# A hybrid decoder layer on one core: where TensorE's operands start, and how the FFN columns are cut

## The chip, the core and the metric

The kernel runs on one core of a Trainium2 chip, as one program in one launch. The metric is the time on the device in microseconds, and the lower one is better. Three runs before the change took 1976.21, 1979.71 and 1979.8 us; the median is 1979.71.

## The reference

One layer on x of 256 tokens by 2048 columns, in float32:

```python
h = x
h = h + 0.5 * swiglu(rms_norm(h, ffn1_norm), w_gate1, w_up1, w_down1)
p = rms_norm(h, mix_norm) @ w_in
h = h + concat([rwkv7_time_mix(p[:, :3360]), rglru_mix(p[:, 3360:])]) @ w_out
h = h + 0.5 * swiglu(rms_norm(h, ffn2_norm), w_gate2, w_up2, w_down2)
out = rms_norm(h, final_norm)
# swiglu(x, g, u, d) = (silu(x @ g) * (x @ u)) @ d
```

The FFNs are 5632 columns wide (11 x 512). The mixer between them has two recurrences over the tokens. Its own code is not touched by the change.

## The kernel before, in words

Every large product is made in three parts. An operand is split into a float32r tile `hi` and the rest `lo`, and hi x hi, hi x lo and lo x hi are added in PSUM. The weights come from DRAM through `weights` (L47): SP issues a DMA of 1 MB into a tile `wst`, of which there are three; ACT casts it to `whi` (L73), DVE subtracts and writes `wlo` (L74), each at most 1024 columns, three tiles of each. `rows_times` (L85) then makes one k (128 rows of the weights): for both row tiles of 128 tokens and each cut of up to 512 columns, the activations are the stationary operand (128 x 128) and the weights the moving one.

`ffn` (L164) cuts the 5632 columns into chunks of 1024, 1024, 1024, 1024, 768 and 768. For each chunk it makes gate over 16 k, then silu on ACT, then up over 16 k, then their product `hid` on DVE. `hidden_T` (L178) turns `hid` with TensorE transposes inside the next chunk's gate (the last chunk's inside the down projection) and splits it into hThi and hTlo. A 768 wide chunk has a cut of 512 and one of 256. After the chunks comes the down projection over 44 k.

The first FFN's stationary operand is `xa` (xahi, xalo), made by `transposed_half` (L126): TensorE transposes x, four blocks for each pair of a k and a PSUM bank half, ACT scales and rounds into xahi (L143), DVE writes the rest into xalo (L144). x comes in four DMAs of 512 columns. The second FFN's stationary operand is `xb`. In the mixer's projections, `columns_times` (L97), the roles are swapped: the weights are stationary, and 256 tokens of xa move.

A scheduler sets the order on each engine, by priorities that the code gives (`high_priority`: the larger offset goes first) and by `issue_after`, which keeps an instruction behind another on its queue.

Where a tile starts follows from the sizes of the tiles before it. In the built program the constants (identity and ones of 512 bytes per partition, gains of 192, `junk` of 2048, small ones) end 22,400 bytes into a partition, and the weights' pool starts there: 1920 bytes past a multiple of 2048. The weights' tiles, xa, h, hT and `hid` all have sizes that keep this remainder, so all of them start 1920 past. The tiles of the right side are packed from the other end: there xb and the second h start 2016 past. Within xa and xb a stationary slice starts at a further multiple of 512, within the weights' tiles a moving one at a multiple of 2048 (with the 768 wide chunks too, one k to a tile).

Of the kernel before, what the change touches and what calls it, by code (L numbers as in the profile page):

```python
# [3 lines left out]

# [7 lines left out]
F32 = mybir.dt.float32  # L12
# [8 lines left out]
class Core:  # L21


    def __init__(self, ctx, tc, S, D, WMAX):
        self.tc, self.nc = tc, tc.nc
        self.S, self.D = S, D
        self.NT, self.NK = S // P, D // P
        self.WMAX = WMAX
        self.const = ctx.enter_context(tc.tile_pool(name="const", bufs=1))
        self.wpool = ctx.enter_context(tc.tile_pool(name="wpool", bufs=3))  # L30
        self.psum = ctx.enter_context(tc.tile_pool(name="psum", bufs=1, space=PSUM))
        self.uid = 0
# [3 lines left out]
        self.h = None  # L36
        self.ones = self.const.tile([P, P], F32, name="ones")
        nc.gpsimd.memset(self.ones, 1.0)
# [7 lines left out]

    def weights(self, pieces, ktiles, kstep=2, kop=1, head=False):  # L47


        nc = self.nc  # L50
        width = sum(w for _, _, w in pieces)
        steps = [1, 1] if head else []
        while sum(steps) < len(ktiles):
            steps.append(min(kstep, len(ktiles) - sum(steps)))
        for k0, n in zip(itertools.accumulate([0] + steps), steps):
            with self.tc.high_priority(offset=4000):
                st = self.wpool.tile([P, 2 * self.WMAX], F32, name=self.name("wst"), tag="wst")
                stv = st[:, : n * width].rearrange("p (k f) -> p k f", k=n)
                kk = ktiles[k0]
                at = 0  # L60
                for mat, c0, w in pieces:
                    nc.sync.dma_start(
                        out=stv[:, :, at : at + w],
                        in_=mat[kk * P : (kk + n) * P, c0 : c0 + w].rearrange("(k p) f -> p k f", p=P),
                    )
                    at += w
                parts = []
                for j in range(0, n, kop):
                    m = min(kop, n - j)
# [3 lines left out]
                    self.last_split = nc.scalar.copy(hi[:, : m * width], src)  # L73
                    nc.vector.tensor_tensor(  # L74
                        lo[:, : m * width], src, hi[:, : m * width].bitcast(F32), ALU.subtract
                    )
                    parts.append((hi, lo))
# [7 lines left out]
    def rows_times(self, banks, xhi, xlo, kidx, whi, wlo, width, first, last):  # L85

        nc = self.nc
        for t in range(self.NT):
# [5 lines left out]
            for n, c, w in cuts:  # L94
                nc.tensor.matmul(banks[t][n][:, :w], b, whi[:, c : c + w], start=False, stop=last)  # L95

# [28 lines left out]

    def transposed_half(self, hf, gT, xhi, xlo, banks):  # L126

        nc = self.nc
        per = self.NK // 2
        for j in range(0, per, 2):  # L130
            bk = self.bank(banks[(j // 2) % len(banks)])
            for jj in range(2):
                k = hf * per + j + jj
                for t in range(self.NT):
                    nc.tensor.transpose(  # L135
                        bk[:, jj * 256 + t * P : jj * 256 + (t + 1) * P],
                        self.h[:, t, k * P : (k + 1) * P],
                        self.ident,
                    )
            for jj in range(2):  # L140
                k = hf * per + j + jj
                src = bk[:, jj * 256 : jj * 256 + self.S]
                nc.scalar.activation(xhi[:, k, :], src, AF.Copy, scale=gT[:, k : k + 1])  # L143
                nc.vector.scalar_tensor_tensor(  # L144
                    xlo[:, k, :], src, gT[:, k : k + 1], xhi[:, k, :].bitcast(F32), ALU.mult, ALU.subtract
                )

    def sumsq(self, c0, w, acc, junk):
# [14 lines left out]

def ffn(core, xhi, xlo, rstd, wg, wu, wd, after_first, after_down, fpool, down, head=False):  # L164
    nc, NT, NK, D, S = core.nc, core.NT, core.NK, core.D, core.S
# [3 lines left out]
    while c < DFF:  # L169
        left = DFF - c  # L170
        w = 1024 if left >= 2 * 1024 or left <= 1024 else left // 2
        w = min(w, left)
        chunks.append((c, w))
        c += w
# [22 lines left out]
    for c0, w in chunks:  # L197
        nb = (w + 511) // 512
        cuts = [(n, n * 512, min(512, w - n * 512)) for n in range(nb)]
        gb = [[core.bank(t * nb + n) for n in range(nb)] for t in range(NT)]  # L200
        for i, (k, hi, lo) in enumerate(core.weights([(wg, c0, w)], ks, head=head and c0 == 0)):
            core.rows_times(gb, xhi, xlo, k, hi, lo, w, i == 0, i == NK - 1)
            if i == NK // 2 - 1:
                for f in pending:
# [20 lines left out]
    for piece, (c0, w) in enumerate(down):  # L225
        nb = w // 512
        db = [[core.bank((bank0 + t * nb + n) % 8) for n in range(nb)] for t in range(NT)]
        bank0 += NT * nb
        for i, (k, hi, lo) in enumerate(core.weights([(wd, c0, w)], list(range(NF)), 2048 // w, 1024 // w)):
            core.rows_times(db, hT_hi, hT_lo, k, hi, lo, w, i == 0, i == NF - 1)  # L230
# [17 lines left out]
class Mix:  # L248
# [170 lines left out]
    def project(self, pieces, ntile, xhi, xlo):  # L419
# [6 lines left out]
        for i, (k, hi, lo) in enumerate(core.weights(pieces, list(range(NK)), 4, 2)):  # L426
            core.columns_times(bks, ntile, i, i == NK - 1, xhi, xlo, k, hi, lo)
# [481 lines left out]
def kernel(ctx: ExitStack, tc: tile.TileContext, dram: dict, out: bass.AP):  # L909
# [23 lines left out]
    def norm_half(i, hf, xhi, xlo):  # L933
        core.transposed_half(hf, gT[:, i * NK : (i + 1) * NK], xhi, xlo, (0, 1, 2, 3) if hf == 0 else (4, 5, 6, 7))

# [11 lines left out]
    with ExitStack() as front:  # L947
        xa = xt_pool(front, "xa")
        with ExitStack() as st:
# [19 lines left out]
            def park(hf):  # L969
# [5 lines left out]
            ffn(core, *xa, rstd[0], dram["ffn1_w_gate"][0], dram["ffn1_w_up"][0], dram["ffn1_w_down"][0],  # L975
                first_norm, park, fpool, [(0, HD), (HD, HD)], head=True)
# [66 lines left out]
```

## Time and profile before

| what | us |
|---|---|
| median of the runs | 1979.71 |
| profiled execution | 1979.79 |
| its span, first to last instruction | 1978.1 |
| PE busy (matmuls) | 1952.5 |
| DVE busy | 1078.4 |
| ACT busy | 880.1 |
| head, to the first product | 12.7 |
| first FFN, gate and up | 496.3 |
| second FFN, gate and up | 504.0 |

The stages follow each other on TensorE: gate and up of the first FFN from 12.7 to 509.0, its down projection to 751.7, the mixer to 1122.8, the output projection to 1221.7, gate and up of the second FFN to 1725.7, its down projection to 1966.2. Matmuls are pipelined, so the duration of one overlaps the next; what a matmul costs is read from the start of one to the start of the next, or from a whole stretch over its count.

### The profile page before, as it was taken

How to read it: one execution, taken by the hardware profiler on the slowest of the kernel's cores; microseconds unless marked ns; L12 is line 12 of the kernel's file. 1: busy time of each engine (PE TensorE's matmuls, PEld its weight loads, DVE VectorE, ACT ScalarE, POOL GpSimd, SP SyncE). 2: the span in 40 equal slices, each digit the busy share in tenths (PEclk: the TensorE clock that was granted, in tenths of full speed). 3: DMA queues.
4: the chain of work that ended last, by engine and by line, in shares of the span. 5: the costliest groups of instructions: out<-in, count | busy, mean ns of one | idle time of the engine just before them, and what ended most of it. 6: DMA issues, size and time to landing. Idle time of an engine off the chain costs nothing.

```text
span 1978.1 us, 26035 instructions
## 1 busy us (share of the span) xinstructions
PE 1952.5 (99%) x10789; PEld 1652.5 (84%) x10789; DVE 1078.4 (55%) x1313; ACT 880.1 (44%) x1062; POOL 8.9 (0%) x52
## 2 busy tenths in 40 slices
PE   8999999999999999999999999999999999999997
PEld 6888888888888889898899878888888888888886
DVE  4455444544545447886684875444545455544543
ACT  4544434444434335544354554434443444443443
POOL 0000000000000001000000000000000000000000
PEclk9999999999999999999999999999999999999999
DMA  6555555566656556544342365555555556665553
GB/s 234 192 189 194 182 196 181 167 189 180 209 187 211 191 187 219 164 139 126 97 147 88 127 224 183 189 192 174 188 187 175 181 175 178 207 214 193 193 192 128
DMA packets 128639, 354.51 MB, mean 179 GB/s; under 512 B 21023, under 2 KB 23272, under 8 KB 128392
## 3 DMA queue, kind: packets, MB, share of 16 engines
q1 hardware_dynamic: 128200, 351.79, 55.4%
q8 instruction: 84, 1.38, 0.3%
q10 hardware_dynamic: 320, 1.06, 0.1%
q14 instruction: 35, 0.29, 0.0%
HBM read 347.05 MB, written 5.77 MB: 178 GB/s over the span
## 4 chain that ended last, share of the span: by engine, by line
PE 97%; DVE 1%; ACT 1%; DMA 0%; issue 0%; SPq 0%; DVEq 0%; ACTq 0%
PE bank L92 26%; PE bank L95 26%; PE bank L93 26%; PE bank L104 4%; PE bank L106 4%; PE bank L105 4%; PE bank L183 1%; PE bank L574 1%; PE bank L502 1%; PE bank L467 0%; PE bank L663 0%; PE bank L135 0%; PE bank L691 0%; PE bank L670 0%; DMA wst<-in_ffn_w_gate_dram 0%
## 5 line engine op out<-in xcount | busy, mean ns | idle before, releaser
L74 DVE TENSOR_TENSOR wlo<-wst,whi 128x1024 fp32r<-128x1024 f32 (+1 forms) x680 | 795.5, 1170 | 834.1 <-ACT whi L73 832.9
L73 ACT CAST whi<-wst 128x1024 fp32r<-128x1024 f32 (+1 forms) x680 | 685.8, 1009 | 1004.5 <-PE bank L95 867.3
L92 PE MATMUL bank<-whi,xahi 128*128 128x512 f32 (+1 forms) x896 | 337.2, 377 | 3.8 <-DVE xalo L144 3.6
L93 PE MATMUL bank<-wlo,xahi 128*128 128x512 f32 (+1 forms) x896 | 330.1, 375 | 1.1 <-DVE wlo L74 1.1
L92 PE MATMUL bank<-whi,xbhi 128*128 128x512 f32 (+1 forms) x768 | 289.5, 377 | 0.0
L93 PE MATMUL bank<-wlo,xbhi 128*128 128x512 f32 (+1 forms) x768 | 283.7, 377 | 0.0
L92 PE MATMUL bank<-whi,hThi 128*128 128x512 f32 x704 | 274.2, 390 | 0.0
L93 PE MATMUL bank<-wlo,hThi 128*128 128x512 f32 x704 | 274.0, 389 | 0.0
L95 PE MATMUL bank<-whi,xalo 128*128 128x512 f32 (+1 forms) x896 | 264.8, 376 | 0.0
L95 PE MATMUL bank<-whi,hTlo 128*128 128x512 f32 x704 | 231.4, 389 | 0.0
L95 PE MATMUL bank<-whi,xblo 128*128 128x512 f32 (+1 forms) x768 | 227.6, 377 | 0.0
L92 PEld LDWEIGHTS bank<-whi,xahi 128*128 128x128 f32 x896 | 168.7, 188 | 41.2 <-DVE xalo L144 4.0
L104 PE MATMUL bank<-xahi,whi 128*128 128x256 f32 x688 | 198.6, 289 | 1.0 <-DVE raw L437 1.0
L106 PE MATMUL bank<-xahi,wlo 128*128 128x256 f32 x688 | 197.4, 288 | 0.0
L105 PE MATMUL bank<-xalo,whi 128*128 128x256 f32 x688 | 196.8, 286 | 0.0
L93 PEld LDWEIGHTS bank<-wlo,xahi 128*128 128x128 f32 x896 | 168.6, 188 | 31.9 <-DVE wlo L74 1.5
L95 PEld LDWEIGHTS bank<-whi,xalo 128*128 128x128 f32 x896 | 159.8, 189 | 24.9
L92 PEld LDWEIGHTS bank<-whi,xbhi 128*128 128x128 f32 x768 | 144.5, 188 | 34.3
L93 PEld LDWEIGHTS bank<-wlo,xbhi 128*128 128x128 f32 x768 | 144.4, 188 | 28.7
L95 PEld LDWEIGHTS bank<-whi,xblo 128*128 128x128 f32 x768 | 135.8, 189 | 23.4
L92 PEld LDWEIGHTS bank<-whi,hThi 128*128 128x128 f32 x704 | 132.2, 188 | 27.4
L93 PEld LDWEIGHTS bank<-wlo,hThi 128*128 128x128 f32 x704 | 132.2, 188 | 27.3
(242 smaller groups left out, 1355.3 us busy)
## 6 DMA issues: line engine op xcount, KB each, us to landing
wst<-in_ffn_w_down_dram SPq DMA_DIRECT2D x88, 1024.0 KB, 5.0
wst<-in_ffn_w_up_dram SPq DMA_DIRECT2D x64, 1024.0 KB, 5.0
wst<-in_ffn_w_gate_dram SPq DMA_DIRECT2D x63, 1024.0 KB, 5.0
wst<-in_w_in_dram SPq DMA_DIRECT2D x40, 1024.0 KB, 5.2
wst<-in_ffn_w_gate_dram SPq DMA_DIRECT2D x32, 768.0 KB, 4.4
wst<-in_ffn_w_up_dram SPq DMA_DIRECT2D x32, 768.0 KB, 4.4
wst<-in_w_out_dram SPq DMA_DIRECT2D x16, 1024.0 KB, 5.5
wst<-in_w_in_dram SPq DMA_DIRECT2D x4, 640.0 KB, 4.3
```

The lines of the kernel that those rows point to most:

```text
L73: self.last_split = nc.scalar.copy(hi[:, : m * width], src)
L74: nc.vector.tensor_tensor(lo[:, : m * width], src, hi[:, : m * width].bitcast(F32), ALU.subtract)
L92: nc.tensor.matmul(banks[t][n][:, :w], a, whi[:, c : c + w], start=first, stop=False)
L93: nc.tensor.matmul(banks[t][n][:, :w], a, wlo[:, c : c + w], start=False, stop=False)
L95: nc.tensor.matmul(banks[t][n][:, :w], b, whi[:, c : c + w], start=False, stop=last)
L104: nc.tensor.matmul(out, a, xhi[:, k, :], start=first, stop=False, skip_group_check=True)
L105: nc.tensor.matmul(out, a, xlo[:, k, :], start=False, stop=False, skip_group_check=True)
L106: nc.tensor.matmul(out, b, xhi[:, k, :], start=False, stop=last, skip_group_check=True)
L183: nc.tensor.transpose(bk[:, jj * 256 + t * P : jj * 256 + (t + 1) * P], hid[:, t, (j + jj) * P : (j + jj + 1) * P], core.ident,)
L502: self.nc.tensor.matmul(bk[0:8, :256], ind[:, j0 + j, :], src[:, j * 256 : (j + 1) * 256], start=j == 0, stop=j == 3)
L574: nc.tensor.matmul(bks[par][:, j * P : (j + 1) * P], BK[j // 2][rows, j % 2, c, :], KR[j // 2][rows, j % 2, c, :], start=True, stop=True,)
```

## The change

Three edits are made together.

- Placement: `junk` is 64 bfloat16 elements longer (128 bytes), so that the weights' pool and what follows it start at multiples of 2048 bytes; the second h gets 504 more elements (2016 bytes), so that xb does too. The constants (the identity), and the mixer's own tiles aren't moved to such multiples.
- Chunks: the 5632 columns are cut into 512 and five of 1024. A 512 wide chunk puts two k into one `whi`/`wlo` tile and four k into one DMA; `weights` works this out from the width. Elsewhere its steps stay as they were.
- Head: the first two k of the first gate come as DMAs of one k each, then one of two k; they are asked for alternately with x's quarters, weights first. x is transposed by quarters (`transposed`): the first before the first product, each later one behind the products of k0, k1 and k2 in turn. The splits of k1 to k7 are kept behind the xahi and xalo of given quarters (`marks`).

```diff
-    def weights(self, pieces, ktiles, kstep=2, kop=1, head=False):
+    def weights(self, pieces, ktiles, head=False):
         width = sum(w for _, _, w in pieces)
-        steps = [1, 1] if head else []
+        kop = self.WMAX // width
+        kstep = 2 * kop
+        steps = [1, 1, 2] if head else []
...
-            with self.tc.high_priority(offset=4000):
+            with self.tc.high_priority(offset={0: 9500, 1: 8700, 2: 8500}.get(k0, 4000) if head else 4000):
...
+                    with ExitStack() as behind:
+                        if head and 0 < k0 < 8:
+                            for mark in self.marks[4 * k0 - 1 if k0 < 3 else -1]:
+                                behind.enter_context(self.tc.issue_after(mark.ins))
...
-        left = DFF - c
-        w = 1024 if left >= 2 * 1024 or left <= 1024 else left // 2
-        w = min(w, left)
+        w = (DFF - c) % 1024 or 1024
...
+            if head and c0 == 0 and i in head:
+                with core.tc.high_priority(offset=3000), core.tc.issue_after(core.last_mm.ins):
+                    head[i]()
...
-    junk = const.tile([P, HD], mybir.dt.bfloat16, name="junk")
+    junk = const.tile([P, HD + 64], mybir.dt.bfloat16, name="junk")
...
-                with tc.high_priority(offset=8000 if q < 2 else 0):
+                with tc.high_priority(offset=(9000, 8600, 8400, 8300)[q]):
...
-            with tc.high_priority(offset=8500):
-                norm_half(0, 0, *xa)
-            norm_half(0, 1, *xa)
+            def norm_quarter(q):
+                core.transposed(4 * q, 4, gT[:, :NK], *xa, ((2, 3), (4, 5), (6, 7))[q % 3])
+
+            with tc.high_priority(offset=8800):
+                norm_quarter(0)
...
-        core.h = h2.tile([P, core.NT, D], F32, name="h2")
+        core.h = h2.tile([P, core.NT * D + 504], F32, name="h2")[:, : core.NT * D].rearrange("p (t d) -> p t d", t=core.NT)
```

On SP, the queue of the DMAs, the program begins before with two quarters of x (`h<-in_x`), then weights (`wst`; the sizes are partitions x k x columns):

```order
L958 DMA h_109<-in_x_dram 128x2x512 x2
L62 DMA wst_197<-in_ffn_w_gate_dram 128x1024
L62 DMA wst_215<-in_ffn_w_gate_dram 128x1024
L62 DMA wst_233<-in_ffn_w_gate_dram 128x2x1024
L958 DMA h_109<-in_x_dram 128x2x512
```

and after the change, with the two gains' loads (`graw`) at its end:

```order
L66 DMA wst_141<-in_ffn_w_gate_dram 128x512
L967 DMA h_109<-in_x_dram 128x2x512
L66 DMA wst_171<-in_ffn_w_gate_dram 128x512
L967 DMA h_109<-in_x_dram 128x2x512
L66 DMA wst_201<-in_ffn_w_gate_dram 128x2x512
L967 DMA h_109<-in_x_dram 128x2x512 x2
L66 DMA wst_237<-in_ffn_w_gate_dram 128x4x512
L66 DMA wst_271<-in_ffn_w_gate_dram 128x4x512
L937 DMA graw_348<-in_mix_norm_dram 16x128
L66 DMA wst_305<-in_ffn_w_gate_dram 128x4x512
L937 DMA graw_353<-in_ffn_norm_dram 16x128
```

Weights and x alternate, and all of x is asked for before the weights of k4; the second gain's load stands in front of the first weights of up.

On TensorE, the program begins before with sixteen transposes (`h` against the identity, banks 119 to 146) and the products of k0 (bank 193 is the first of the gate's four):

```order
L135 MATMUL bank_119<-ident,h_109 128x128 x4
L135 MATMUL bank_128<-ident,h_109 128x128 x4
L135 MATMUL bank_137<-ident,h_109 128x128 x4
L135 MATMUL bank_146<-ident,h_109 128x128 x4
L92 MATMUL bank_193<-whi_199,xahi 128x512
```

and after the change with eight (banks 139 and 140 are the gate's two; `whi_143` is k0):

```order
L142 MATMUL bank_119<-ident,h_109 128x128 x4
L142 MATMUL bank_128<-ident,h_109 128x128 x4
L100 MATMUL bank_139<-whi_143,xahi 128x512
L101 MATMUL bank_139<-wlo_144,xahi 128x512
L103 MATMUL bank_139<-whi_143,xalo 128x512
L100 MATMUL bank_140<-whi_143,xahi 128x512
L101 MATMUL bank_140<-wlo_144,xahi 128x512
L103 MATMUL bank_140<-whi_143,xalo 128x512
L142 MATMUL bank_153<-ident,h_109 128x128 x4
L142 MATMUL bank_162<-ident,h_109 128x128 x4
```

Half as many transposes stand in front of the first product, and the next quarter's stand between k0 and k1.

Some rows further on TensorE, after the change, around the end of k3 (`whi_203`) and the start of k4 (`whi_239`), the gains' transposes (`graw`) stand among the products:

```order
L103 MATMUL bank_140<-whi_203,xalo 128x512
L939 MATMUL bank_350<-ident,graw_348 128x16
L100 MATMUL bank_139<-whi_239,xahi 128x512
L100 MATMUL bank_140<-whi_239,xahi 128x512
L939 MATMUL bank_355<-ident,graw_353 128x16
L101 MATMUL bank_139<-wlo_240,xahi 128x512
```

Before, both stood after the first gate stage; now the second gain's is in front of k4's second product.

## Rows read from the trace of the kernel before

**Rows 1.** The page: busy us (share), and the chain that ended last, by engine.

```profile
PE 1952.5 (99%) x10789; PEld 1652.5 (84%) x10789; DVE 1078.4 (55%) x1313; ACT 880.1 (44%) x1062; POOL 8.9 (0%) x52
...
PE 97%; DVE 1%; ACT 1%; DMA 0%; issue 0%; SPq 0%; DVEq 0%; ACTq 0%
```

**Rows 2.** PE's busy time by stage (length, busy, clock, DMA share, GB/s).

```profile
core 0: us, PE busy (x), PEclk, DMA share, GB/s
12.70:60.60 47.90, 47.90 (x210) 1.00 0.61 208
327.60:371.10 43.50, 43.50 (x193) 1.00 0.56 176
...
406.50:440.30 33.80, 33.80 (x195) 1.00 0.64 187
1268.50:1313.50 45.00, 45.00 (x193) 1.00 0.58 187
...
1623.90:1657.40 33.50, 33.50 (x195) 1.00 0.65 189
509.00:630.10 121.10, 121.10 (x543) 1.00 0.57 191
1846.80:1906.60 59.80, 59.80 (x265) 1.00 0.58 193
```

**Rows 3.** Groups of PE by line and shape, second FFN's gate and up (busy, mean ns).

```profile
L92 PE MATMUL bank<-whi,xbhi 128*128 128x512 f32 x640 | 253.5, 396 | 0.0
```

**Rows 4.** The chain of waits in the head (start, length in us).

```profile
1.80 6.60 DMA wst<-in_ffn_w_gate_dram
8.42 1.05 ACT whi L73
9.50 0.41 DVE wlo L74
...
12.25 0.41 DVE xalo L144
12.70 0.79 PE bank L92
13.49 0.43 PE bank L93
...
17.66 0.23 PE bank L92
```

**Rows 5.** Timelines of PE, ACT and DVE in the head; the gains' load.

```profile
5.10 4.01 PE L135 MATMUL bank<-ident,h 128*128 128x128 f32 x16 [1.09 <-DMA h<-in_x_dram]
...
9.37 0.47 ACT L143 ACTIVATE xahi<-bank,gT 128x256 fp32r<-128x256 f32 x1
13.21 0.83 ACT L143 ACTIVATE xahi<-bank,gT 128x256 fp32r<-128x256 f32 x2
25.22 1.05 ACT L73 CAST whi<-wst 128x1024 fp32r<-128x1024 f32 x1
...
9.50 1.23 DVE L74 TENSOR_TENSOR wlo<-wst,whi 128x1024 fp32r<-128x1024 f32 x1 [5.28 <-ACT whi L73]
10.64 0.48 DVE L144 SCALAR_TENSOR_TENSOR xalo<-bank,gT,xahi 128x256 fp32r<-128x256 f32 x1
...
DMA to landing us min/median/max: 2.8/2.8/2.8
```

**Rows 6.** The chain of waits: one chunk's transposes of the hidden rows.

```profile
126.59 1.75 PE bank L183 x16
```

**Rows 7.** Timeline of PE in a projection of the mixer, first and last of 27.

```profile
802.80 0.28 PE L106 MATMUL bank<-xahi,wlo 128*128 128x256 f32 x1
802.92 0.28 PE L104 MATMUL bank<-xahi,whi 128*128 128x256 f32 x1
...
805.92 0.28 PE L105 MATMUL bank<-xalo,whi 128*128 128x256 f32 x1
```

**Rows 8.** All engines' busy time in a stretch of the head (last: GB/s).

```profile
4.00:6.00 2.00, 0.91 (x5) 0.91 (x5) 0.17 (x1) 0.00 (x0) 0.00 (x0) 1.00 0.98 339
```

More of the change, by code (lines that the diff above doesn't have):

```diff
@@ L3 @@
 from contextlib import ExitStack
+from functools import partial
 import concourse.bass as bass
@@ L36, in __init__ @@
         self.h = None
+        self.marks = []
         self.ones = self.const.tile([P, P], F32, name="ones")
@@ L72, in weights @@
                     lo = self.wpool.tile([P, self.WMAX], F32R, name=self.name("wlo"), tag="wlo")
[L73 to L76, printed above, removed]
+                    with ExitStack() as behind:
+                        if head and 0 < k0 < 8:
+                            for mark in self.marks[4 * k0 - 1 if k0 < 3 else -1]:
+                                behind.enter_context(self.tc.issue_after(mark.ins))
+                        self.last_split = nc.scalar.copy(hi[:, : m * width], src)
+                        nc.vector.tensor_tensor(
+                            lo[:, : m * width], src, hi[:, : m * width].bitcast(F32), ALU.subtract
+                        )
                     parts.append((hi, lo))
@@ L94, in rows_times @@
             for n, c, w in cuts:
-                nc.tensor.matmul(banks[t][n][:, :w], b, whi[:, c : c + w], start=False, stop=last)
+                self.last_mm = nc.tensor.matmul(banks[t][n][:, :w], b, whi[:, c : c + w], start=False, stop=last)
     def columns_times(self, bks, ntile, i, last, xhi, xlo, k, hi, lo):
@@ L124, in spread_rstd, with transposed @@
         nc.vector.tensor_copy(self.rb, bk[:, :256])
-    def transposed_half(self, hf, gT, xhi, xlo, banks):
+    def transposed(self, k0, n, gT, xhi, xlo, banks):
         nc = self.nc
-        per = self.NK // 2
-        for j in range(0, per, 2):
+        for j in range(0, n, 2):
             bk = self.bank(banks[(j // 2) % len(banks)])
             for jj in range(2):
-                k = hf * per + j + jj
+                k = k0 + j + jj
                 for t in range(self.NT):
@@ L140, in transposed_half @@
             for jj in range(2):
-                k = hf * per + j + jj
+                k = k0 + j + jj
                 src = bk[:, jj * 256 : jj * 256 + self.S]
-                nc.scalar.activation(xhi[:, k, :], src, AF.Copy, scale=gT[:, k : k + 1])
-                nc.vector.scalar_tensor_tensor(
+                a = nc.scalar.activation(xhi[:, k, :], src, AF.Copy, scale=gT[:, k : k + 1])
+                b = nc.vector.scalar_tensor_tensor(
                     xlo[:, k, :], src, gT[:, k : k + 1], xhi[:, k, :].bitcast(F32), ALU.mult, ALU.subtract
                 )
+                self.marks.append((a, b))
     def sumsq(self, c0, w, acc, junk):
@@ L161, in rstd_of, with ffn @@
         nc.vector.reciprocal(rstd, tmp)
-def ffn(core, xhi, xlo, rstd, wg, wu, wd, after_first, after_down, fpool, down, head=False):
+def ffn(core, xhi, xlo, rstd, wg, wu, wd, after_first, after_down, fpool, down, head=None):
     nc, NT, NK, D, S = core.nc, core.NT, core.NK, core.D, core.S
@@ L200, in ffn @@
         gb = [[core.bank(t * nb + n) for n in range(nb)] for t in range(NT)]
-        for i, (k, hi, lo) in enumerate(core.weights([(wg, c0, w)], ks, head=head and c0 == 0)):
+        for i, (k, hi, lo) in enumerate(core.weights([(wg, c0, w)], ks, head=bool(head) and c0 == 0)):
             core.rows_times(gb, xhi, xlo, k, hi, lo, w, i == 0, i == NK - 1)
+            if head and c0 == 0 and i in head:
+                with core.tc.high_priority(offset=3000), core.tc.issue_after(core.last_mm.ins):
+                    head[i]()
             if i == NK // 2 - 1:
@@ L228, in ffn @@
         bank0 += NT * nb
-        for i, (k, hi, lo) in enumerate(core.weights([(wd, c0, w)], list(range(NF)), 2048 // w, 1024 // w)):
+        for i, (k, hi, lo) in enumerate(core.weights([(wd, c0, w)], list(range(NF)))):
             core.rows_times(db, hT_hi, hT_lo, k, hi, lo, w, i == 0, i == NF - 1)
@@ L425, in project @@
             self.nproj += 1
-        for i, (k, hi, lo) in enumerate(core.weights(pieces, list(range(NK)), 4, 2)):
+        for i, (k, hi, lo) in enumerate(core.weights(pieces, list(range(NK)))):
             core.columns_times(bks, ntile, i, i == NK - 1, xhi, xlo, k, hi, lo)
@@ L933, in norm_half @@
     def norm_half(i, hf, xhi, xlo):
-        core.transposed_half(hf, gT[:, i * NK : (i + 1) * NK], xhi, xlo, (0, 1, 2, 3) if hf == 0 else (4, 5, 6, 7))
+        core.transposed(hf * NK // 2, NK // 2, gT[:, i * NK : (i + 1) * NK], xhi, xlo, (0, 1, 2, 3) if hf == 0 else (4, 5, 6, 7))
     def norm_rows(i, bank):
@@ L975 @@
             ffn(core, *xa, rstd[0], dram["ffn1_w_gate"][0], dram["ffn1_w_up"][0], dram["ffn1_w_down"][0],
-                first_norm, park, fpool, [(0, HD), (HD, HD)], head=True)
+                first_norm, park, fpool, [(0, HD), (HD, HD)], head={q: partial(norm_quarter, q + 1) for q in range(3)})
         mix_layer(core, dram, *xa, scratch, NSLOT)
```

## The prediction

> **What bounds the kernel now.** I read the page first, for the share of each engine and of the chain that ended last: TensorE is busy for 99% of the span, and PE holds 97% of the chain [rows 1]. So the time is the sum of what each matmul keeps TensorE, and little else counts. I then read the busy time stage by stage, where each stretch runs from a stage's first matmul to the next stage's first [rows 2]. The duration shown for one matmul (396 ns, [rows 3]) overlaps its neighbours and is no cost; the cost is the length of a stage over its number of matmuls. Three prices come out.
>
> - An up stage of the first FFN, 1024 columns wide, has 16 k by 2 row tiles by 2 column cuts by 3 products, 192 matmuls of 512 columns, in 43.5 us [rows 2]: 226.6 ns each. The down projection gives the same: 264 matmuls in 59.8 us, 226.5 ns.
> - The same stage of the second FFN takes 45.0 us: 234.4 ns each, 7.8 ns more for the same instruction count. The weights' tiles are the same ones. What differs is the stationary operand, xb instead of xa, which begins 2016 bytes past a multiple of 2048 where xa begins 1920 past.
> - An up stage of a 768 wide chunk has 96 matmuls of 512 and 96 of 256 columns and takes 33.8 us in the first FFN and 33.5 us in the second [rows 2]. At the 512 price, its work would be 144 matmuls, 32.6 us.
>
> Last I read the chain from the start to the first products, and beside it the engines' own instructions there [rows 4, 5]: TensorE starts them at 12.70, and the first stage of 192 ends at 60.6. 43.5 us of that are products, so the head costs 17.1 us.
>
> **FFN columns in 512 and 5x1024.** Each FFN's gate and up have 2 x 11 x 96 = 2112 matmuls of 512 after the change. Before they have 1536 of 512 and 384 + 384 in the four narrow stages; 384 matmuls go in the whole program. In the first FFN before: 8 x 43.5 + 4 x 33.8 = 483.2 us; after: 2112 x 226.6 ns = 478.6 us. That is -4.6 us, all on the path, since no engine but TensorE is waited for in these stages. The transposes of the hidden rows stay 88 per FFN (16 in 1.75 us [rows 6]); of the last chunk's, 16 instead of 12 come later, beside the down projection, which only moves them.
>
> **Operands on multiples of 2048 bytes.** Nothing in the trace has both operands there, so the price per matmul must be bounded. From above: 234.4 ns, the dearest placement shown. From below: the same matmul takes 0.43 us at 13.49 and 0.23 at 17.66 [rows 4]; the first is TensorE's lower level of 1.2 GHz by its length (the granted clock reads 1.00 there as later [rows 2], so that record doesn't show it), and half of it, 215 ns, is what the columns alone need at 2.4 GHz. I take 226.6 ns for all. The reason: in the first FFN moving and stationary operand start at the same distance from a multiple of 512, and so they do after the change; in the second they are 96 bytes apart, and this goes. So xb's stages fall to xa's price, and nothing shows that xa's stages gain. Second FFN: before 8 x 45.0 + 4 x 33.5 = 494.0 us, after 478.6 us: -15.4 us. Of this 12 us come from the address and 3.4 us from the chunks.
>
> The trace speaks of one more stage: the mixer's projections run 256 columns in 0.12 us [rows 7], and 27 in a row keep that step, more than two k, though the moving slice starts 1920 bytes past a multiple of 2048 for an even k, and so crosses the next one, and 896 past for an odd k, and doesn't. So a moving operand that crosses a multiple of 2048 is not dearer in itself. I count the mixer at no change.
>
> The Trainium skill, "TensorE: Matmul & The Clock Gate", section "Back-to-back issue gap", gives an isolated gap of N/2.4 + 2.5 ns, 216 ns for 512 columns, at whatever address. The trace doesn't agree: its best stage stands at 226.5. Were it what operands on 2048 get, the time would be as in the first rival.
>
> **The head.** Its orders change on four queues, and every piece is small against TensorE's 17.1 us there.
>
> - SP asks for 256 KB of weights, then x's first quarter. Before, the first quarter (512 KB) let the transposes start at 5.10 [rows 5]. DMA moves 339 GB/s then [rows 8], so 256 KB ahead of it cost some 0.7 us: start at 5.8. Eight transposes instead of sixteen (4.01 us) end at 7.8; the weights' cast and split are half as wide and already done, and the first xahi and xalo (0.47 and 0.48 us) fall beside the last transposes. The first product stands at about 7.8, not 12.7.
> - What is late next: the quarter behind. k0 takes six matmuls at 0.43 us, to 10.4. The second quarter's 1.5 MB in all have landed by 8, its transposes run to 12, k1 to about 14. The split of k2 and k3 stands behind the second quarter's four xahi (0.42 us each) and xalo on ACT and DVE, then cast 1.05 and split 1.23: done at about 15.8, TensorE waits 1.2 us. The third and fourth quarter push the next split to 21.6 in the same way: some 2 us more.
> - A new wait: gain 2's load stands on SP behind gain 1's transpose (after k3, about 19.7), and with 2.8 us to land [rows 5] TensorE, where its transpose now stands inside k4, waits to about 22.6. Queued behind it are all products of k4.
> - From there 70 of the 96 products of the first chunk remain: 15.9 us, end at 38.6. Less 96 x 226.6 ns = 21.8 us, the head costs 16.8 us against 17.1: -0.3 us.
>
> Bounds: -4.8 us, if no quarter waits (first product at 7.8, 2 us at the lower clock, 2.6 us for 24 transposes); +3 us, if each split behind a quarter holds TensorE 1 us longer. The earlier start is mostly given back in waits because the work of ACT and DVE on x is the same.
>
> The first stage now lasts 21.8 us instead of 43.5, and four sums of squares and two table loads must be done on ACT before the silu. Casts need 1.05 us of each 2.72 us in which TensorE uses one; some 9 us of extra work fit in five or six such periods, and three tiles of each split are ahead. I count nothing; if that cover is gone, it is the rest of one such period, under 2 us for each FFN, inside the range.
>
> **Sum.** The profiled execution took 1979.79 us, and the median of the runs is 1979.71, so I work from 1979.8. -4.6 - 15.4 - 0.3 = -20.3: **1959.5 us**, 1.0% faster. Its own range is 1954 to 1966 (head -4.8 to +3, the per-matmul price within half a nanosecond of 226.6).
>
> **Rivals.**
>
> - *The surcharge falls further.* What a matmul takes over 215 ns is a matter of addresses, and on 2048 it goes. For: the trace shows that an address moves the price by 7.8 ns, and xa's 1920 is no special number. Against: the stages of xa and hT all stand at 226.5 to 226.9, and the mixer's two offsets agree. 6720 matmuls of 512 remain (4224 in gate and up, 2112 in down, 384 in the output projection) x 11.6 = 78 us, and the 2064 of the mixer at most 0.012 us each, 25 us, half of it off the path: 1959.5 - 78 - 12 = 1870. If half of the surcharge goes: 1915.
> - *The place, not the address.* xb lies in another part of the memory, and that makes it dear. Then the second FFN stays at 234.4: 2112 x 234.4 = 495.0 against 494.0, and the time is 1979.8 - 4.6 - 0.3 + 1.0 = 1976. For: the trace can't separate the two. Against: hTlo of the first FFN lies at the same end of the memory, across xb's place, and its down projection pays 226.9 (121.1 us less 1.3 us for 12 transposes, over 528 [rows 2]).
> - The Trainium skill, "SBUF - State Buffer", section "Door 1: The DMA port swizzle", counts access by lines of 16 bytes; 1920 and 2016 are both multiples of 16, so by that rule the start can't matter, and the time would be that of this second rival.
> - *Slower: a common start is the dear case.* With weights, activations and hidden rows all on multiples of 2048, the streams of TensorE, ACT and DVE fall on the same phase, and all 512 column matmuls pay 234.4: 6720 x 7.8 = 52 us on top, 2012 us. It decides from 20.3 us / 6720 = 3 ns, so from 229.6 ns per matmul. For: no row shows a common multiple. Against: in every stage ACT and DVE already read and write at the weights' own phase (1920), and TensorE doesn't show it.
>
> **Chances.** Forecast 0.55; surcharge gone 0.11, half gone 0.13; the place 0.11; slower 0.08; something else in the head 0.02. The range should hold the forecast, the place at 1976 and half the surcharge at 1915 and somewhat below: 1892 to 1977. It leaves out the whole surcharge and the slower case, 0.19. A change under 0.2% (4 us) can't be told from none here; the place lies on that edge, half of it on either side. Faster: 0.55 + 0.24 + 0.06 = 0.85; same 0.06; slower, with half of what is left of the head, 0.09.
>
> **What would show it.** In the profile after, an up stage of 1024 columns of the second FFN should last 43.5 us, one of the first FFN too, and the 512 wide ones 21.8. If the first FFN's last below 42.5, the first rival holds; if the second FFN's stay at 45, the place does; if both are at 45, the common start is dear. The head: first product near 7.8, and the end of the first gate stage near 38.6. The forecast is wrong if stage lengths of xa move at all.

## The result, and the profile after

The changed kernel took 1957.23 us (median of four runs, 1955.79 to 1959.1), the kernel before beside it 1979.68 (1976.21 to 1979.8). The ratio is 0.9891, with a 95% interval of 0.9874 to 0.9908, so the change is faster by 1.1%. The forecast was 1959.5 us. The profiled execution took 1957.12 us.

Line numbers have moved: the FFN's three products are L100, L101 and L103 (before L92, L93, L95), the mixer's L112 to L114, the cast and the split of the weights L81 and L82, xahi and xalo L150 and L151.

The page answers to [rows 1]: busy us with share of the span and instructions, and the chain that ended last.

```profile
PE 1929.5 (99%) x10405; PEld 1628.8 (83%) x10405; DVE 1073.3 (55%) x1278; ACT 874.9 (45%) x1027; POOL 8.9 (0%) x52
...
PE 97%; DVE 1%; ACT 1%; DMA 0%; issue 0%; SPq 0%; DVEq 0%; ACTq 0%
```

TensorE has 384 instructions less and is as full as before: the time still is the sum of what the matmuls keep it.

The stages of after, against [rows 2] (length, PE busy, granted clock, DMA share, GB/s):

```profile
core 0: us, PE busy (x), PEclk, DMA share, GB/s
7.89:37.50 29.61, 26.71 (x125) 1.00 0.73 258
37.50:59.20 21.70, 21.70 (x97) 1.00 0.59 194
281.20:324.80 43.60, 43.60 (x194) 1.00 0.59 193
1303.90:1347.40 43.50, 43.50 (x193) 1.00 0.59 193
1824.10:1883.90 59.80, 59.80 (x265) 1.00 0.57 194
7.89:502.40 494.51, 491.61 (x2213) 1.00 0.59 194
745.50:1115.20 369.70, 365.41 (x3400) 1.00 0.46 141
1214.10:1702.70 488.60, 488.60 (x2202) 1.00 0.58 190
```

The fourth line is what the prediction hung on: a 1024 wide up stage of the second FFN lasts 43.5 us, where it had 45.0. The first FFN's stay at 43.5 to 43.6, its 512 wide one takes 21.7, and the down projection's 264 matmuls keep 59.8. The whole gate and up of the second FFN falls from 504.0 to 488.6 us.

The group that answers to [rows 3] (busy us, mean ns):

```profile
L100 PE MATMUL bank<-whi,xbhi 128*128 128x512 f32 x704 | 274.3, 390 | 0.0
```

The duration shown for one fell from 396 to 390 ns, which is what xa's show; it overlaps the neighbours now as before.

The chain of waits in the head, against [rows 4] (start, length):

```profile
6.21 1.97 PE bank L142 x8
8.18 0.51 PE bank L100
8.69 0.43 PE bank L101
...
9.48 0.23 PE bank L100
...
13.56 1.24 DVE wlo L82
...
18.78 2.43 DMA graw<-in_ffn_norm_dram
```

And TensorE's own waits there, from its timeline, against [rows 5] (start, length, instruction, in brackets the idle time before it and what ended it):

```profile
7.89 0.80 PE L100 MATMUL bank<-whi,xahi 128*128 128x512 f32 x1
...
14.84 0.50 PE L101 MATMUL bank<-wlo,xahi 128*128 128x512 f32 x1 [0.53 <-DVE wlo L82]
...
19.43 0.74 PE L100 MATMUL bank<-whi,xahi 128*128 128x512 f32 x2 [0.68 <-ACT whi L81]
21.34 0.20 PE L939 MATMUL bank<-ident,graw 16*128 16x16 f32 x1 [1.17 <-DMA graw<-in_ffn_norm_dram]
21.47 0.50 PE L101 MATMUL bank<-wlo,xahi 128*128 128x512 f32 x1
```

The first product stands at 7.89. Then TensorE waits where the prediction had put it: for the cast and the split of k2 and k3 (0.28 and 0.53 us), for the cast of k4, and for the second gain, whose transpose is in front of k4's second product.

Where the 22.9 us of the span went (1978.1 to 1955.2), by the stages' starts in both profiles: gate and up of the first FFN with the head 6.6 less (509.0 to 502.4), its down projection 0.4 more, the mixer 1.4 less (371.1 to 369.7), the output projection 98.9 in both, gate and up of the second FFN 15.4 less, its down projection, from its first to its last matmul, 0.4 more, what follows it 0.2 less.

### The profile page after: what moved, and what is told of

It is laid out like the page before. It is cut to its first block, busy times and chain, and to the rows that moved or that the text cites. A ratio compares the mean times of both kernels' runs of the same rounds, so it can differ in the third digit from the quotient of the medians.

```text
span 1955.2 us, 25119 instructions
## 1 busy us (share of the span) xinstructions
PE 1929.5 (99%) x10405; PEld 1628.8 (83%) x10405; DVE 1073.3 (55%) x1278; ACT 874.9 (45%) x1027; POOL 8.9 (0%) x52
## 4 chain that ended last, share of the span: by engine, by line
PE 97%; DVE 1%; ACT 1%; DMA 0%; issue 0%; SPq 0%; DVEq 0%; ACTq 0%
PE bank L101 26%; PE bank L103 26%; PE bank L100 26%; PE bank L112 4%; PE bank L114 4%; PE bank L113 4%; PE bank L189 1%; PE bank L583 1%; PE bank L511 1%; PE bank L476 0%; PE bank L142 0%; PE bank L672 0%; PE bank L700 0%; PE bank L679 0%; DVE wlo L82 0%
## 5 line engine op out<-in xcount | busy, mean ns | idle before, releaser
L82 DVE TENSOR_TENSOR wlo<-wst,whi 128x1024 fp32r<-128x1024 f32 (+1 forms) x649 | 790.2, 1218 | 820.1 <-ACT whi L81 818.9
L81 ACT CAST whi<-wst 128x1024 fp32r<-128x1024 f32 (+1 forms) x649 | 680.5, 1049 | 985.2 <-PE bank L103 843.2
L101 PE MATMUL bank<-wlo,xahi 128*128 128x512 f32 x832 | 324.2, 390 | 1.6 <-DVE wlo L82 1.6
L100 PE MATMUL bank<-whi,xahi 128*128 128x512 f32 x832 | 324.6, 391 | 1.2 <-ACT whi L81 1.0
L100 PE MATMUL bank<-whi,xbhi 128*128 128x512 f32 x704 | 274.3, 390 | 0.0
L100 PE MATMUL bank<-whi,hThi 128*128 128x512 f32 x704 | 274.2, 389 | 0.0
L101 PE MATMUL bank<-wlo,xbhi 128*128 128x512 f32 x704 | 274.1, 389 | 0.0
L101 PE MATMUL bank<-wlo,hThi 128*128 128x512 f32 x704 | 274.0, 389 | 0.0
L103 PE MATMUL bank<-whi,xalo 128*128 128x512 f32 x832 | 262.9, 390 | 0.0
L103 PE MATMUL bank<-whi,hTlo 128*128 128x512 f32 x704 | 231.3, 389 | 0.0
L103 PE MATMUL bank<-whi,xblo 128*128 128x512 f32 x704 | 222.1, 389 | 0.0
L112 PE MATMUL bank<-xahi,whi 128*128 128x256 f32 x688 | 198.4, 289 | 1.0 <-DVE raw L446 1.0
L114 PE MATMUL bank<-xahi,wlo 128*128 128x256 f32 x688 | 197.1, 287 | 0.0
L101 PEld LDWEIGHTS bank<-wlo,xahi 128*128 128x128 f32 x832 | 156.4, 188 | 34.6 <-DVE wlo L82 2.5
L100 PEld LDWEIGHTS bank<-whi,xahi 128*128 128x128 f32 x832 | 156.3, 188 | 34.4 <-ACT whi L81 1.3
L103 PEld LDWEIGHTS bank<-whi,xalo 128*128 128x128 f32 x832 | 156.2, 188 | 32.3
L100 PEld LDWEIGHTS bank<-whi,hThi 128*128 128x128 f32 x704 | 132.2, 188 | 27.3
L103 PEld LDWEIGHTS bank<-whi,xblo 128*128 128x128 f32 x704 | 132.2, 188 | 27.3
L103 PEld LDWEIGHTS bank<-whi,hTlo 128*128 128x128 f32 x704 | 132.1, 188 | 27.4
L101 PEld LDWEIGHTS bank<-wlo,hThi 128*128 128x128 f32 x704 | 132.2, 188 | 27.2
L101 PEld LDWEIGHTS bank<-wlo,xbhi 128*128 128x128 f32 x704 | 132.2, 188 | 27.1
```

What stands on the lines that cost most here:

```text
L82: nc.vector.tensor_tensor(lo[:, : m * width], src, hi[:, : m * width].bitcast(F32), ALU.subtract)
L100: nc.tensor.matmul(banks[t][n][:, :w], a, whi[:, c : c + w], start=first, stop=False)
L101: nc.tensor.matmul(banks[t][n][:, :w], a, wlo[:, c : c + w], start=False, stop=False)
L103: self.last_mm = nc.tensor.matmul(banks[t][n][:, :w], b, whi[:, c : c + w], start=False, stop=last)
L112: nc.tensor.matmul(out, a, xhi[:, k, :], start=first, stop=False, skip_group_check=True)
L114: nc.tensor.matmul(out, b, xhi[:, k, :], start=False, stop=last, skip_group_check=True)
```

## The experiments

The theory was the prediction's: a 512 wide matmul is dear when its moving and its stationary operand start at unequal distances from some boundary, cheap when they start at equal ones. Rivals were the place of xb in memory, the absolute alignment on 2048, and, for the first FFN, a gain of the common start beyond xa's price.

### The chunks alone

The kernel before, with the chunk rule and the steps from the width alone:

```diff
...
-        left = DFF - c
-        w = 1024 if left >= 2 * 1024 or left <= 1024 else left // 2
-        w = min(w, left)
+        w = (DFF - c) % 1024 or 1024
...
```

> The kernel before with the new chunks alone (512 and 5x1024); addresses and head order as before. Theory of the sum: the first FFN's gate and up lose 4.6 us (2112 matmuls at 226.6 ns against 483.2 us), the second FFN's keep xb's dear price and gain nothing (2112 x 234.4 = 495.0 against 494.0 us), so 1979.7 - 4 = about 1976. An up stage of 1024 columns: 43.5 us in the first FFN, 45.0 in the second. Rival, that the narrow chunks were what made the second FFN slow: both FFNs gain, 1968 or less.

It took 1975.74 us against 1976.52 of before (ratio 0.9989, 0.998 to 0.9999). The runs of before spread from 1975.91 to 1980.36, so a few us show better in the stages:

```profile
105.10:148.60 43.50, 43.50 (x194) 1.00 0.59 194
1308.40:1353.40 45.00, 45.00 (x194) 1.00 0.57 187
```

The second FFN's up stage keeps its 45.0 us: the chunks don't take the surcharge away. The first FFN's gate and up end at 503.9 instead of 509.0.

### xb at the weights' own start, 1920

The kernel before, with 96 bytes more behind the second h, so that xb starts 1920 past a multiple of 2048 like the weights:

```diff
-        core.h = h2.tile([P, core.NT, D], F32, name="h2")
+        core.h = h2.tile([P, core.NT * D + 24], F32, name="h2")[:, : core.NT * D].rearrange("p (t d) -> p t d", t=core.NT)
```

> The kernel before with one edit: the second h is 96 bytes longer, so that xb starts 1920 bytes past a multiple of 2048, like the weights and xa, and none of them on a multiple. Theory, that the distance between the two operands (or half a 64) is the price and the multiple of 2048 is not: the wide up stages of the second FFN fall from 45.0 to 43.5 us, 1979.7 - 12 = about 1968. Rival, that only a multiple of 2048 helps: 45.0 us stay, 1979.7.

1967.43 us against 1976.52 of before, ratio 0.9949 (0.9933 to 0.9964). The same up stage, and the whole gate and up of the second FFN:

```profile
1267.20:1310.70 43.50, 43.50 (x194) 1.00 0.59 193
1221.70:1715.00 493.30, 493.30 (x2397) 1.00 0.59 187
```

A move by 96 bytes, with xb still in the same part of the memory and nothing on 2048, gives the whole 1.5 us per wide stage. So the place falls, and the multiple of 2048 isn't needed. The whole gate and up falls from 504.0 to 493.3 us, 10.7 and not the 12 expected: the narrow up stages, 33.5 us before [rows 2], take 33.8 now, as in the first FFN.

### Everything 32 bytes past

The kernel after, with `junk` 16 elements (32 bytes) longer still and the second h's pad 496 instead of 504: weights, xa, hT and xb start 32 past.

```diff
-    junk = const.tile([P, HD + 64], mybir.dt.bfloat16, name="junk")
+    junk = const.tile([P, HD + 80], mybir.dt.bfloat16, name="junk")
...
```

> The changed kernel with every operand 32 bytes past a multiple of 2048: weights, xa, xb and hidden rows alike, so the distance between moving and stationary operand is a multiple of 512 as in the changed kernel. Theory A, the price goes by the distance between the two: wide up stages 43.5 us in both FFNs, 1957. Theory B, each start must be a multiple of 64 bytes by itself: 45.0 us in both FFNs and the down projections too, 1957 + 6720 x 7.8 ns = about 2009.

1958.86 us in one run, and both FFNs at 43.5:

```profile
105.20:148.70 43.50, 43.50 (x194) 1.00 0.58 194
1305.50:1349.00 43.50, 43.50 (x193) 1.00 0.59 193
```

So it is the distance between the two operands, with starts at 0, 32 and 1920 alike. Of the 1.7 us over the profiled execution of after, 1.5 lie in the head, whose first gate ends at 39.0 (37.5), with eleven matmuls at 426 to 427 ns in this execution.

### The distance, in four steps

Each is the kernel after with a small tile in front of xa (16, 64, 48, 40 floats) and another pad behind the second h, so that xa, with the first hT, and xb start some bytes past where the weights start. For the first:

```diff
+        front.enter_context(tc.tile_pool(name="xpad", bufs=1)).tile([P, 16], F32, name="xpad")
...
-        core.h = h2.tile([P, core.NT * D + 504], F32, name="h2")[:, : core.NT * D].rearrange("p (t d) -> p t d", t=core.NT)
+        core.h = h2.tile([P, core.NT * D + 496], F32, name="h2")[:, : core.NT * D].rearrange("p (t d) -> p t d", t=core.NT)
```

xa 64 bytes past, xb 32:

> The changed kernel with the weights on 2048, xa and the first FFN's hidden rows 64 bytes past and xb 32 bytes past. Theory A with a period of 64 bytes, and theory B (multiples of 64): wide up stages 43.5 us in the first FFN, 45.0 in the second, its down projection unmoved, so 1957 + 2112 x 7.8 ns = about 1974. Theory A with a longer period: 45 us in the first FFN too, its down projection longer by 1056 x 7.8 ns = 8 us, about 1999.

xa 256 past, xb 128:

> The changed kernel with xa and the first FFN's hidden rows 256 bytes past a multiple of 2048, xb 128 past, weights on it. Theory A, the distance between moving and stationary operand counts, with a period that 64 bytes is not a multiple of (64 gave 233.3 ns, 0 gave 226.6): with a period of 128 bytes both FFNs have 43.5 us in a wide up stage; with 256 the first FFN 43.5 and the second another price; with 512 neither has 43.5. Rival, any distance but 0 costs 233.3 ns: 44.8 us in both FFNs, 1957 + (4224 + 1056 + 384) x 6.7 ns = about 1995.

xa 192 past, xb 224:

> The kernel after, but xa and the first hT start 192 bytes past a multiple of 2048 and xb 224 past (the weights and the second hT stay at 0). Known by now: distance 0 or 256 between stationary and moving start costs 226.6 to 226.9 ns per 512 wide matmul, 32, 64 and 128 cost 233.3, 233.3 and 232.4, and the old -96 (moving minus stationary the other way round: stationary 96 further) 234.4. Theory A: any distance that is not a multiple of 256 bytes costs the same 232 to 234 ns, so the first FFN's up stages take 44.6 to 44.9 us and the second's too, and the time is 1957 + (2112 + 1056 + 384 + 2112) x 6.5 ns = 1994 (hT of the second FFN stays at 226.7). Rival B: the price has a finer shape (192 is 64 before the next multiple of 256, 224 is 32 before it); a distance just before a multiple is cheap or cheaper than 226.6: then one of the two stages stays at 43.5 us or falls, and the time is 1975 or less. The mixer's projections: at distance 64 they ran 117 to 118 ns per 256 wide matmul and at 0, 128 bytes away or 256, 120; if the mixer follows the distance with the sign turned, 192 gives another value than 120.

xa 160 past, xb 192:

> The kernel after, but xa and the first hT start 160 bytes past a multiple of 2048 and xb 192. If the price falls evenly from distance 128 (232.4 ns) to 192 (228.9), the first FFN's 512 wide matmuls cost some 230.7 ns (up stages 44.3 us) ; xb at 192 should give 228.9 as xa did (44.0 us). Time then 1957.2 + 3552 x 4.0 ns + 2112 x 2.2 ns = 1976. Rival: 192 was something of xa alone (its stages also follow the tiles' places), then xb at 192 costs 232 to 234, 44.6 us or more. The mixer at 160: between 113 and 120 ns per 256 wide matmul, no better estimate.

The times of one run each: 1992.89, 1969.51, 1978.78 and 1980.64 us. The 1024 wide up stages of the first and of the second FFN, in this order of the kernels (192 matmuls in each):

```profile
105.80:150.60 44.80, 44.80 (x194) 1.00 0.57 188
1328.10:1372.90 44.80, 44.80 (x194) 1.00 0.57 188
```

```profile
103.60:147.10 43.50, 43.50 (x193) 1.00 0.60 194
1306.30:1351.00 44.70, 44.70 (x194) 1.00 0.57 188
```

```profile
104.50:148.40 43.90, 43.90 (x193) 1.00 0.58 192
1314.20:1359.00 44.80, 44.80 (x194) 1.00 0.57 188
```

```profile
105.30:150.00 44.70, 44.70 (x193) 1.00 0.58 188
1323.50:1367.40 43.90, 43.90 (x193) 1.00 0.59 191
```

From the starts of the matmuls against xa and xb, one costs:

| stationary start less moving start, bytes | 0 | 32 | 64 | 96 (before) | 128 | 160 | 192 | 224 | 256 |
|---|---|---|---|---|---|---|---|---|---|
| ns per 512 wide matmul | 226.7 | 233.3 | 233.3 | 234.4 | 232.4 | 233.3 | 228.9 | 233.3 | 226.7 |

256 bytes cost nothing, 128 nearly all: the distance counts modulo 256, as far as these nine go (beyond 256 none was run, but for the multiples of 512 between the slices of one tile). The hidden rows agree: with xa and the first hT 64 bytes past, the first FFN's down projection takes 249.9 us instead of 243.1. A period of 64, one of the two expected answers of the first of these runs, falls. Of the answers expected for 192 and 224 neither came: 192 is cheaper than the others and still dearer than 0, 224 is dear, and the time lies between the two expected. The even fall between 128 and 192 that the last one expected is wrong too (160 costs 233.3, not 230.7; 1980.64 us instead of 1976); but 192 gave 228.9 for xa and for xb alike, so it is no matter of the tile.

### The order of the head alone

The kernel after with before's order of the head (weights in steps of 1, 1 and then 4 k, x in halves):

```diff
...
-            with tc.high_priority(offset=8800):
-                norm_quarter(0)
+            with tc.high_priority(offset=8500):
+                norm_half(0, 0, *xa)
+            norm_half(0, 1, *xa)
...
```

> The changed kernel with the head of before (x in halves, weights behind x, no marks), new chunks and addresses kept. Prediction's step: the new head was worth -0.3 us, bounds -4.8 to +3; the profile after put it at -1.4. So the end of the first gate (37.4 us) should stand at 37.5 to 39 us, and the time at 1957 to 1959. Rival, the head did a real part of the gain: 1960 or more.

1959.4 us, ratio to before 0.9901 (0.9884 to 0.9917), where after has 0.9891 (0.9874 to 0.9908). The two intervals overlap, so only the profile can tell them apart: the first gate, from the first product, and the first up:

```profile
11.14:38.00 26.86, 26.55 (x113) 1.00 0.68 234
38.00:60.30 22.30, 22.30 (x98) 1.00 0.59 190
```

With the new order these end at 37.5 and 59.2. It starts products 3.25 us earlier and ends 0.5 us earlier; another 0.6 us is gained in the up stage, which takes 21.7 instead of 22.3. No wait is in that (TensorE is busy throughout in both): with before's order a gain's transpose stands among its first products, which step by up to 0.34 us there, and with the new order both gains' transposes are through by k4. So the head's order is worth 1.1 us, in one profile of each.

### The wait for the second gain taken away

The three gains are loaded at the start into one tile on ACT's queue and transposed at once:

```diff
-                load_gain(0, fpool, nc.scalar)
+                raw = fpool.tile([3 * NK, P], F32, name="graw", tag="sg")
+                for i in range(3):
+                    nc.scalar.dma_start(out=raw[i * NK : (i + 1) * NK, :], in_=dram[gains[i]][0].rearrange("(k p) -> k p", p=P))
...
-                for i in (1, 2):
-                    load_gain(i, fpool, nc.sync)
...
```

> The changed kernel with all three gains loaded at the start into one tile and transposed at once, so that no gain's transpose stands among the products of k3 and k4. TensorE's idle 1.17 us before the second gain's transpose goes, and the split of k4 is the next to be late (it ends at 20.6 us against 21.47): about 1 us earlier at the end of the first gate, 36.4 instead of 37.4. Rival, three loads on ACT's queue delay its table load and the first cast, and k0 starts later by as much.

1960.04 us in one run. TensorE's timeline in the head:

```profile
6.68 0.31 PE L967 MATMUL bank<-ident,graw 48*128 48x48 f32 x1 [6.68 <-DMA graw<-in_ffn_norm_dram]
...
21.37 0.73 PE L100 MATMUL bank<-whi,xahi 128*128 128x512 f32 x2 [1.13 <-ACT whi L81]
22.63 0.61 PE L101 MATMUL bank<-wlo,xahi 128*128 128x512 f32 x1 [0.53 <-DVE wlo L82]
23.05 0.63 PE L103 MATMUL bank<-whi,xalo 128*128 128x512 f32 x1
23.47 0.63 PE L101 MATMUL bank<-wlo,xahi 128*128 128x512 f32 x1
```

The expected 1 us didn't come. The wait of 1.17 us for the gain is gone, but TensorE now waits 1.13 us for the cast of k4 and 0.53 for its split, where it had waited 0.68 for the cast. The gains' transpose starts at 6.68, where the first gain's stood at 3.30, and the first product stands at 8.59, 0.7 us later. That k0 would start later the rival had said, but not by way of the first cast, which starts at 3.62 (3.57 in after). And after the two waits matmuls step by 0.43 us, until 26, before they step by 0.23 again, with a granted clock of 0.95 over the stage. It ends at 40.2 instead of 37.5.

A second execution of the changed kernel itself (the run of it further down) shows the same place without these side effects, because there the gain landed in time:

```profile
19.89 0.73 PE L100 MATMUL bank<-whi,xahi 128*128 128x512 f32 x2 [0.98 <-ACT whi L81]
20.74 0.20 PE L939 MATMUL bank<-ident,graw 16*128 16x16 f32 x1
21.14 0.50 PE L101 MATMUL bank<-wlo,xahi 128*128 128x512 f32 x1 [0.20 <-DVE wlo L82]
```

TensorE waits for the cast and the split of k4; the second product comes 0.33 us sooner than at 21.47, and the first gate ends at 37.2. So the wait for the gain partly covered that for the next tiles that are late. An estimate of what it cost is 0.3 us, from this execution, to 0.9, the time by which k4's split (done at 20.6 in the first execution) was ahead of the gain.

### The mixer's matmuls, made cheaper

In the runs with xa at 64 and at 192 the mixer's 256 wide matmuls, where xa moves and the weights are stationary, had become *faster* than at distance 0: 117 to 118 ns, and mostly 113 to 114 (at 160 the mean is 118, at 256 it is 120 again). So the kernel after got xa tiles 256 bytes longer and two views of them: one at 0, for the 512 wide products, and one 192 bytes further, written before the mixer and read by its projections.

```diff
...
-        xa = xt_pool(front, "xa")
+        xa, xm = xt_two(front, "xa", 48)
...
-                norm_half(1, hf, *xa)
+                norm_half(1, hf, *xm)
...
-        mix_layer(core, dram, *xa, scratch, NSLOT)
+        mix_layer(core, dram, xm, xa, scratch, NSLOT)
...
```

> The kernel after, but the mixer's projections read xa from a view that starts 192 bytes past a multiple of 256 (the xa tiles are 256 bytes longer, park writes the shifted view, split_rows the unshifted one), while all 512 wide products keep distance 0. With xa at 192 throughout, the mixer took 366.5 us instead of 369.7 and its 256 wide matmuls mostly stepped by 113 ns instead of 120, but the FFN and the output projection paid 228.9 ns. Theory A, the distance is a matter of the two operands of one product: both gains hold together, FFN stages stay at 226.7 ns, the mixer takes 366.5, and the time is 1957.2 - 3.2 = 1954.0, ratio to before 0.9870. Rival: the mixer is bound by its chain of other engines and the lower step of TensorE was a chance of the order, then 1957 within 1.

1956.35 us (1954.34 to 1956.48), ratio to before 0.9885 (0.9868 to 0.9901). That is 0.9 us under the changed kernel's 1957.23 and can't be told from it. So both ran once more, side by side:

> The changed kernel itself, once more, beside the next one on the same chip: 1957.2 within 1, ratio to before 0.989.

> The kernel with the mixer's view of xa 192 bytes further, again, beside the one above. If the mixer's 3 us hold (366.7 against 369.7 us in the profiled executions), 1954.2 and 3 us below the one above. Rival: the gain of the profiled execution was one of its order only, and the medians are within 1 us of each other, as those of different chips were (1956.35 and 1957.23).

They took 1956.77 (1955.31 to 1958.56; ratio 0.9897, 0.9881 to 0.9913) and 1956.32 us (1954.98 to 1962.76; 0.9897, 0.988 to 0.9913): no gain can be told. Yet the step is shorter. In the kernel after, 25 steps of the mixer, 0.120 us each (compare [rows 7]):

```profile
796.00 0.28 PE L112 MATMUL bank<-xahi,whi 128*128 128x256 f32 x1
...
799.00 0.28 PE L113 MATMUL bank<-xalo,whi 128*128 128x256 f32 x1
```

With the shifted view, 15 steps, 0.114 us each (seven in ten of the mixer's steps are like these, most others 0.116 to 0.119):

```profile
897.01 0.28 PE L112 MATMUL bank<-xahi,whi 128*128 128x256 f32 x1
...
898.72 0.28 PE L112 MATMUL bank<-xahi,whi 128*128 128x256 f32 x1
```

Part of the gain goes in two places. One is the projection at 885 us, here for after, in two executions:

```profile
885.00:921.80 36.80, 35.78 (x358) 0.95 0.57 166
```

```profile
884.60:920.10 35.50, 34.48 (x359) 1.00 0.57 157
```

and for the shifted view: the whole mixer, this projection, and the first half of the output projection, in its second execution:

```profile
745.30:1111.90 366.60, 358.70 (x3400) 0.99 0.46 142
882.50:921.40 38.90, 36.73 (x359) 0.91 0.55 158
1111.90:1168.90 57.00, 55.26 (x223) 0.94 0.53 183
```

Without this projection the mixer falls by 5.2 us, from 332.9 to 327.7. The projection takes 2.1 to 3.4 us more, at a granted clock of 0.91. Who is waited for there shows in the waits, of after and then of the first execution with the shifted view (total, times, longest):

```profile
PE bank L112 <- DVE raw L446: 1.0, 1, 1.0
```

```profile
PE bank L112 <- DVE raw L446: 2.1, 1, 2.1
```

TensorE comes sooner to a tile that DVE writes and waits 2.1 us instead of 1.0. The rest goes with the clock. The kernel before, with a wait of 1.0 us for this tile too, had the same projection at 0.91:

```profile
891.20:929.40 38.20, 37.18 (x357) 0.91 0.56 163
```

With one and the same wait the clock is 0.91 there, 0.95 or 1.00. So no run shows that the longer wait lowers it; what the clock takes differs between executions of one kernel. The first half of the output projection takes 57.0 us in the second execution with the shifted view, at 0.94 (54.0 in the first, at 1.00), where after has 53.5; why is open. From the mixer's start to the output projection's end, after has 468.6 and 467.1 us, the shifted view 466.1 and 469.0.

## Why the prediction was right

- *The price of a matmul.* Taken at 226.6 ns for all, it is 226.7 in both FFNs. The second FFN's gate and up were to lose 15.4 us and lost 15.4. The prediction split this into 12 us for the address and 3.4 for the chunks, and there it was off: xb's move alone took each wide stage from 45.0 to 43.5 us (12 us over eight) but each narrow one up by 0.3, so 10.7 in all, and the chunks on top of it bring 4.7, as in the first FFN (4.6). The chunks alone left the wide stage at 45.0.
- *The reason.* Equal distance, not a place and not a boundary of its own: shown by moving xb alone by 96 bytes, and by moving everything by 32. The prediction spoke of multiples of 512; the runs say 256. No run shows why.
- *The rivals.* The place falls with xb at 1920. The surcharge doesn't fall below xa's price at any of the nine distances. The common start isn't dear: 0 is the cheapest, with 256. The Trainium skill, "SBUF — State Buffer", section "Door 1: The DMA port swizzle", counts in lines of 16 bytes, by which all these starts are alike; the trace doesn't agree for TensorE's operands, since starts that are all multiples of 32 differ by 7.7 ns. The Trainium skill, "TensorE: Matmul & The Clock Gate", section "Back-to-back issue gap", has an isolated gap of 216 ns for 512 columns; the trace doesn't agree, since no distance here came below 226.5 (59.8 us over 264).
- *The chunks in the first FFN.* -4.6 us by the stages' count; the chunks alone moved the end of gate and up by 5.1, of which the rest is in the head (a first gate of half the length ends at 38.3, and 38.3 - 21.8 = 16.5 against 17.1).
- *The head*, the term that was mis-sized: -0.3 us taken, and the first gate ends at 37.5 instead of 38.6: 37.5 - 21.8 = 15.7 against 17.1 is -1.4 us. The start was right (7.89 for 7.8), and so was what is late next, in its order. The waits were taken too long: 1.2 us for the split of k2 and k3 where cast and split took 0.81, and k4's split done at 21.6 where it was at 20.6. What sets the end is the last one: k4's second product was put at 22.6 and came at 21.47, because k3's products were through earlier, the gain's load was issued at 18.78 and not at 19.7, and it landed in 2.43 us and not 2.8. Only the first products stepped by 0.43 us (0.23 from 9.48), where six had been counted. And of the 1.17 us for the gain only 0.3 to 0.9 are its own price, by the estimate above: without it TensorE waits for the cast and the split of k4.
- *What was costed at nothing.* ACT's extra work in the shorter first stage cost nothing: TensorE has no idle time in the first up, nor in gate and up of the second FFN (busy 488.60 of 488.60). The transposes that moved to the down projections cost 0.4 us in each (four, where 16 take 1.75 [rows 6]), and are taken from the stage they left. The gains' transposes left the surroundings of the first up, where they had cost 0.5 to 0.6 us (44.0 us for the first up before, 43.5 for that FFN's other wide ones); the prediction counted their wait in the first gate and not this. The mixer's 1.4 us are not the change's: the one projection in which they lie took 38.2 us before, 36.8 and 35.5 in two executions of the changed kernel, and 38.1 with before's head order.
- *The sum.* -20.3 taken, -22.4 by the medians, -22.9 by the profiled spans. The rest of the spans is the head (1.1), the first up behind it (0.6) and the mixer's projection (1.4), less the moved transposes (0.8). The mixer's part is chance.

## What to carry to other kernels

Where an engine is full, compare two stages with the same instructions: a few per cent between them can lie in where the operands start, and moving one tile by a few bytes says so. Keep the stationary and the moving operand of a wide float32r matmul at the same start modulo 256 bytes; a larger alignment brought nothing here. An earlier start or a cheaper instruction is worth little by itself when another engine's tile is late next: the wait moves there, as in the head (3.25 us earlier at the start, 0.5 at the end of the first gate).

## What was not expected of the hardware

- The price of a 512 wide float32r matmul depends on the distance of its two operands' starts modulo 256 bytes: 226.7 ns at 0, 228.9 at 192, 232.4 to 234.4 at the other multiples of 32.
- For 256 wide matmuls in the mixer it goes the other way: equal starts are dear, with 120 ns at distance 0 and at 256, and 113 to 114 for most where the moving operand starts 192 bytes past the stationary one. Why it turns round is open.
- Two waits of 1.13 and 0.53 us, one product pair apart, were followed by 3.4 us of matmuls at 0.43 us (1.2 GHz by their length). Their length alone doesn't decide it: with everything 32 bytes past, 0.96 and 0.53 us at the same place were followed by six such matmuls, in the first run with the shifted view 0.98 and 0.54 by none, and in the kernel after 0.68 and 1.17 by none.
